# A fixed number of filler steps per attention slot, a moved fetch, and a new order of weight tiles ahead of the merge

## The chip, the core and the metric

The kernel runs on one core of a Trainium2 chip. Five engines with queues of their own work on it: TensorE (PE in the rows; its weight loads have rows of their own, PEld), VectorE (DVE), ScalarE (ACT), GpSimd (POOL) and SyncE (SP), which here mostly issues DMAs. The metric is the device time of one execution in microseconds, the median of several runs. Times in a profile are counted from the start of the span of one profiled execution.

## The reference, cut to what matters

One block of a conformer-like network, batch 1, 1024 tokens, width 1024, all in float32.

```
h = rms_norm(x, norm1_g);  z = h @ w_in                  # 1024 x 7168
glu_in, q, k, v, gate_logits = split(z)
a = a_val * sigmoid(a_gate)                              # from glu_in
a = silu(rms_norm(causal_depthwise_conv(a, 31 taps)))
y_a = a @ w_conv_out
q, k = rms_norm per head;  q *= 64 ** -0.5               # 16 heads of 64
for window, dilation in ((128, 1), (512, 4), (2048, 16)):
    o_g, lse_g = dilated_window_attention(q, k, v, slopes, window, dilation)
o = sum over g of softmax(lse)_g * o_g
y_b = o @ w_attn_out
g_a, g_b = split(sigmoid(gate_logits + gate_b))
x = x + (g_a * y_a + g_b * y_b) @ w_out
h = rms_norm(x, norm2_g)
u = causal_depthwise_conv(h @ w_up, 3 taps)
return x + (silu(u_gate) * u_val) @ w_down
```

## The kernel before

**Numbers as pairs.** Each float32 operand of a product is split into a high part, rounded to the type float32r by ACT (L83), and a low part, the difference, by DVE (L84). A product is then three matmuls: high x high, high x low, low x high. Weights are loaded by SP into a ring of four buffers, tag `raw` in `stage` (L88), and split into rings of four, `whi` and `wlo`. The rings are shared by everything that stages a tile, so a load waits until an older tile has been split or added.

**Who sets the order.** Blocks under `tc.manual_schedule` keep the order in which the code issues its instructions on ACT, DVE and PE. Everything else, all of SP's DMAs among it, is put in order by a planner when the program is built: an instruction goes out when the planner's own model of the run has its inputs and its buffer ready, earlier code first among those that are ready. On the chip each engine then works through its list strictly in that order. SP has eight DMAs in flight at most; the next one waits for the one eight places before.

**Stages.** First norm and gated convolution input; q, k and v (L132 to L134), spilled to DRAM; the convolution on DVE; then the gates of five pairs of channels by a Strassen-like scheme (`PAIRS`, the loop at L799 and on, products at L139 to L141), with copies out of PSUM into `quarter` buffers (five places in turn) that are written to `dgate` in DRAM; then the attention; then the merge with `w_attn_out`, the output product, and the feed-forward part from about 1100 us on.

**The attention loop.** A slot is one block of 128 queries of one head: 16 heads x 2 halves x 4 blocks, 128 slots, and six more behind. In each slot PE computes the scores (`score`, L887 and L888), issues filler steps, transposes the probabilities of a block five slots older (`flip`, L907, `BACK`), weighs the values with the transposes of the slot before (`weigh`, L921 and L922), and issues more filler steps. DVE adds the mask and finds the row extreme (L892), ACT takes the exponent (L897, in `powers`), and one slot later DVE and POOL divide by the sum (`share`, L900 and L901). ACT and DVE split each transpose into `ph` and `pl` (L83, L84). At the end of a half, `result` copies the output (L930) and writes it to `do_` in DRAM (L932). Later slots of a half have more keys: a score has 128 to 1024 columns.

**Filler steps.** `side_steps` (L195 and on) is a generator over work that does not depend on the attention: four late gate channels (`LATE`) and the eight output channels of `y_a`, in two halves each. One step is three matmuls of 512 columns (`gemm_half`, L115 to L117), eight steps make one half of a channel: (4 + 8) x 2 x 8 = 192 steps. `fill` advances the generator. Its weights are asked for two or three uses ahead, and their splits go through a queue of pieces, one or two a slot. What is left of the generator when the slots are done is issued in one go, the drain:

```
            for _ in gates:
                piece_low()
                piece_high()
```

**The merge.** `load_heads(half)` reads the attention's output back, two arrays per pair of chunks, adds them on DVE (L1008) and splits the sum into `oT`, whose memory lies where the attention's tiles were. `merge(c, w, half)` multiplies it with the tile `ao{c}` of `w_attn_out` and with the gates: channels 0 to 3 for half 0, then the same for half 1, then channels 4 to 7.

Of the kernel before, what the change touches and what calls it, by code (L numbers as in the profile page):

```python
# [32 lines left out]

LAG = 2
WARM = 7
FILL = (0.8, 2.2, 0.6, 0.6, 0.4, 1.7, 0.8, 0.9)
FIRST = 1.0
BACK = 5
SHARE = 0.6
PLAIN = (10, 11)  # L40
LATE = (12, 13, 14, 15)
PAIRS = ((0, 1), (2, 3), (4, 5), (6, 7), (8, 9))
# [15 lines left out]
def block_kernel(ctx: ExitStack, tc: tile.TileContext, x, xT, x0, g2, pack, mask,  # L58
# [27 lines left out]
    def stage(src, name):  # L86
        raw = wp.tile([P, 1024], F32, tag="raw", bufs=4, name=f"raw_{name}")
        sp.dma_start(raw.rearrange("p (a b) -> p a b", a=src.shape[1]) if len(src.shape) == 3 else raw, src)  # L88
        return raw
# [7 lines left out]
    def wpiece(src, name, raw=None):  # L97
        raw = stage(src, name) if raw is None else raw
        hi, lo = wsplit(raw, name)
        if len(src.shape) == 3:  # L100
            hi = hi.rearrange("p (a b) -> p a b", a=src.shape[1])
            lo = lo.rearrange("p (a b) -> p a b", a=src.shape[1])
        return hi, lo
# [45 lines left out]
    def fetch(dst, src):  # L149
        sp.dma_start(dst.bitcast(F32), src.bitcast(F32))  # L150
# [150 lines left out]
    if True:  # L301
# [431 lines left out]
        def head(h):  # L733
            hp, r, g8 = h // 2, (h % 2) * DH, h // 8
            q = p2.tile([P, T], F32R, tag="q", bufs=2, name=f"q_{h}")
            kh = p2.tile([P, T], F32R, tag="kh", bufs=2, name=f"kh_{h}")
            kl = p2.tile([P, T], F32R, tag="kl", bufs=2, name=f"kl_{h}")
            m = p2.tile([P, T], F32, tag="m", bufs=2, name=f"m_{h}")
            for s in range(2):
                fetch(q[s * DH : (s + 1) * DH, :], dq[g8][s][r : r + DH, hp % 4, :])  # L740
                fetch(kh[s * DH : (s + 1) * DH, :], dk[g8][0][r : r + DH, hp % 4, :])
                fetch(kl[s * DH : (s + 1) * DH, :], dk[g8][1][r : r + DH, hp % 4, :])
            sp.dma_start(m, mask[h])
            return q, kh, kl, m
# [6 lines left out]
        tiles = {}  # L751
        tt_ = lambda o, a, b, op: dve.tensor_tensor(out=o, in0=a, in1=b, op=op)

        def load(n, which):
            raws[n][which] = stage(w_ch[16 + PAIRS[n][which]], f"g{which}_{n}")
# [9 lines left out]
        def parts(n, which, name):  # L765
            src = raws[n][which] if which != "s4" else raws[n][0][:, 512:]
            pw[n][name] = [four(t) for t in wsplit(src, f"{name}_{n}")]
# [26 lines left out]
        with tc.manual_schedule(engines=hand):  # L794
            for n in range(2):
                xz[n] = gate_first(n, firsts[n])
                begun(n)
            load(1, 0)
            for n, (a, b) in enumerate(PAIRS):  # L799
                X = xz[n][:, 0:512]  # L800
                Y = bank_ps(f"gy_{n}")
                (sh, sl), (gh, gl) = pw[n]["s12"], pw[n]["s3"]
                inner = 0 < n < N - 1
                if n + 2 < N:
                    load(n + 2, 0)
                if n == 3:
                    p1_cm.__exit__(None, None, None)
                    p2_cm = tc.tile_pool(name="ph2", bufs=1, reuse_waits="tile")
                    p2 = p2_cm.__enter__()
                    pool2.append(p2)  # L810
                    tiles[0] = head(0)
                if n + 1 < N:
                    load(n + 1, 1)
                parts(n, "s4", "s4")
                if inner:
                    parts(n + 1, 0, "v")
                product(X, sh[:, 4:8], sl[:, 4:8], *form["t2"], False)
                c12 = quarter(f"c12_{n}")
                act.activation(c12, X, AF.Copy)
                product(Y, sh[:, 0:4], sl[:, 0:4], *form["t1"], True)  # L820
                p5 = quarter(f"p5_{n}")
                act.activation(p5, Y, AF.Copy)
                if n == 0:
                    rs8 = conv_factors()
                if n == 1:
                    conv_spread(rs8)
                if 0 < n < 3:
                    for c in range(4 * n - 4, 4 * n):
                        conv_result(c)
                product(X, gh[:, 0:4], gl[:, 0:4], *b12, False)  # L830
                c22 = quarter(f"c22_{n}")
                tt_(c22, X, p5, add)
                sp.dma_start(dgate[b][:, 512:1024], c22)
                if n + 1 < N:
                    sums(n + 1)
                if inner:
                    xz[n + 1] = big_ps(f"gx_{n + 1}")
                    for i in range(2):
                        product(xz[n + 1][:, i * 512 : i * 512 + 512], *(t[:, 4 * i : 4 * i + 4] for t in pw[n + 1]["v"]),
                                *left[i], True)  # L840
                    parts(n + 1, 2, "s12")
                    begun(n + 1)
                else:
                    product(Y, *pw[n]["s4"], *b22, False)
                    tt_(c12, Y, c12, add)
                    if n + 1 < N:
                        parts(n + 1, 2, "s12")
                product(X, gh[:, 4:8], gl[:, 4:8], *form["t4"], False)
                c21 = quarter(f"c21_{n}")
                act.activation(c21, X, AF.Copy)  # L850
                sp.dma_start(dgate[b][:, 0:512], c21)
                if inner:
                    product(Y, *pw[n]["s4"], *b22, False)
                if n + 1 < N:
                    parts(n + 1, 1, "s3")
                if inner:
                    tt_(c12, Y, c12, add)
                sp.dma_start(dgate[a][:, 512:1024], c12)
# [7 lines left out]
    if True:  # L866
# [64 lines left out]
            for i in range(2):  # L931
                sp.dma_start(do_[i][r : r + DH, h // 2, cs], tmp[i * DH : (i + 1) * DH, :])  # L932

        credit = [0.0]

        def fill(n):
            credit[0] += n
            while credit[0] >= 1.0:
                credit[0] -= 1.0
                next(gates, None)  # L940

        slots = [(h, half, n) for h in range(H) for half in range(2) for n in range(4)]
        pts = {}
# [7 lines left out]
        with tc.manual_schedule(engines={ENG.Activation, ENG.DVE, ENG.PE}):  # L953
            pend = []
            for at in range(len(slots) + BACK + 1):
                count[2] += 1
                cur = slots[at] if at < len(slots) else None
                rate = FILL[at % 8] + FIRST * (at < 6) if cur else 4
                if cur is not None:
                    h, half, n = cur  # L960
                    if (half, n) == (0, 2) and h + 1 < H:
                        tiles[h + 1] = head(h + 1)
                    if (half, n) == (1, 2) and h + 1 < H:
                        values(h + 1)
                    new = score(h, tiles[h], half * 4 + n)
                    pts[h, half, n] = new[0]
                if late is not None:
                    share(*late)
                if len(pieces) > 2:
                    piece_high(2)  # L970
                fill(rate * SHARE)
                flips = []
                if BACK <= at < len(slots) + BACK:
                    h, half, n = slots[at - BACK]
                    nkt = half * 4 + 4
                    row4 = [pts[h, half, i] for i in range(4)]
                    for kt in range(n * nkt // 4, (n + 1) * nkt // 4):
                        flips.append((h, half, vals[h], *flip(h, half, row4, kt)))
                for w in pend:
                    done = weigh(*w) or done  # L980
                pend = flips
                late = None
                if done is not None:
                    result(*done)
                    done = None
                if cur is not None:
                    powers(*new)
                    late = new
                piece_low()
                fill(rate * (1 - SHARE))  # L990
                piece_high(2)
            for _ in gates:
                piece_low()
                piece_high()
# [7 lines left out]
    if True:  # L1002
# [6 lines left out]
                split(oT[0][half][:, k : k + 2, :], oT[1][half][:, k : k + 2, :], raw.rearrange("p (a b) -> p a b", a=2))  # L1009

        load_heads(0)
        ao_raw = [stage(w_ao[c], f"ao{c}") for c in range(2)]
        load_heads(1)
        mT = hb_tiles(hb1, "mT")
        gb2 = p3.tile([P, D], F32, name="gb2")
# [36 lines left out]

        wo_first = []
        for c0 in (0, 4):
            ws = [wpiece(w_ao[c], f"ao{c}", ao_raw.pop(0) if ao_raw else None) for c in range(c0, c0 + 4)]
            for half in range(2):
                for c in range(c0, c0 + 4):
                    if c < 6 or not half:
                        merge(c, ws[c - c0], half)
# [553 lines left out]
```

## Time and profile before

| | |
|---|---|
| median of three runs | 1748.92 us (1747.99 to 1751.1) |
| the profiled execution | 1752.18 us, its span 1750.1 us |
| PE busy | 1733.1 us, 99% of the span |
| DVE, ACT, POOL busy | 1333.5, 812.6, 174.6 us |
| mean granted clock of PE | 0.998 of full speed |
| DMA over the span | 171 GB/s |

A row of the timeline gives start, duration, engine, line, operation, what is written and read, the shapes, and in brackets the idle time before it with what ended it. SPq and ACTq are DMA issues. Because matmuls are pipelined, a matmul's duration is longer than its distance to the next, and a busy PE can still be waiting for a fraction of a microsecond. Tile names leave their numbers out, so `p<-gy` of L822 is the copy `p5`. `gx` and `gy` are the gate pairs' PSUM tiles, `gate` and `ya` those of filler steps, `yb` that of the merge.

### The profile page before, as it was taken

To read this page: it belongs to the slowest core of one execution; us is meant where nothing else is said; L and a number is where in the kernel's file an instruction comes from. 1 tells how busy PE (TensorE), PEld (TensorE's weight loads), DVE (VectorE), ACT (ScalarE), POOL (GpSimd) and SP (SyncE) were. 2 spreads that over 40 slices of the span, in tenths; PEclk is the share of its full clock that TensorE was granted. 3 is DMA by queue.
4 is the path that set the end of the run, shared out by engine and by line. 5 is a ranking of instruction groups with operands and counts; after the bars stand their busy time and mean duration, and the time that the engine had idled before them with its cause. 6 is when DMAs were issued, how large, how long until landed. Compare 5 with 4: busy or idle time off the path is not lost.

```text
span 1750.1 us, 22916 instructions
## 1 busy us (share of the span) xinstructions
PE 1733.1 (99%) x8147; PEld 1440.5 (82%) x8147; DVE 1333.5 (76%) x2032; ACT 812.6 (46%) x1284; POOL 174.6 (10%) x188
## 2 busy tenths in 40 slices
PE   9999999999999899999999999999999999999999
PEld 7888888888878788888888888888888888888887
DVE  5999999999875467776755564787776777789863
ACT  5421233323444477877755442555544544544431
POOL 0000231131000133333310000000000000000000
PEclk9999999999999999999999999999999999999999
DMA  9311145345547768876749577632222222399851
GB/s 376 134 57 51 50 133 169 113 140 168 175 165 231 254 181 218 233 230 187 194 127 323 174 258 259 214 117 85 85 84 85 79 91 84 125 339 329 294 175 49
DMA packets 159842, 299.02 MB, mean 171 GB/s; under 512 B 13296, under 2 KB 63088, under 8 KB 159216
## 3 DMA queue, kind: packets, MB, share of 16 engines
q1 hardware_dynamic: 157280, 291.14, 51.2%
q10 hardware_dynamic: 2448, 6.42, 0.9%
q8 instruction: 64, 1.05, 0.2%
q14 instruction: 50, 0.41, 0.1%
HBM read 213.62 MB, written 83.89 MB: 170 GB/s over the span
## 4 chain that ended last, share of the span: by engine, by line
PE 93%; DMA 3%; DVE 2%; issue 1%; ACT 0%; SPq 0%; POOL 0%; ACTq 0%; DVEq 0%
PE dx L1425 7%; PE xz L139 6%; PE xz L141 6%; PE xz L140 6%; PE dy L1425 5%; PE qkv L134 5%; PE qkv L132 5%; PE qkv L133 5%; PE pp L907 4%; PE y L141 2%; PE y L139 2%; PE y L140 2%; PE o L922 2%; PE s L888 2%; PE s L887 2%; PE o L921 2%
## 5 line engine op out<-in xcount | busy, mean ns | idle before, releaser
L132 PE MATMUL qkv<-hi_qkv,hT 128*128 128x512 f32 x384 | 151.2, 395 | 0.0
L134 PE MATMUL qkv<-hi_qkv,hT 128*128 128x512 f32 x384 | 149.8, 391 | 0.0
L133 PE MATMUL qkv<-lo_qkv,hT 128*128 128x512 f32 x384 | 149.8, 391 | 0.0
L84 DVE TENSOR_TENSOR pl<-pp,ph 128x512 fp32r<-128x512 f32 (+2 forms) x191 | 99.5, 549 | 46.5 <-ACT ph L83 46.5
L1328 DVE SCALAR_TENSOR_TENSOR u<-u,pk 128x1023 f32<-128x1023 f32 x88 | 112.3, 1278 | 1.2 <-ACT u L1326 0.9
L901 POOL TENSOR_SCALAR p<-p,st 128x128 f32<-128x128 f32 (+3 forms) x120 | 89.3, 747 | 196.4 <-DVE st L900 137.2
L892 DVE CUSTOM_DVE_ANT_0 p<-s,m 128x128 f32<-128x128 f32 (+3 forms) x120 | 90.3, 753 | 24.1 <-PE pp L907 20.4
L83 ACT ACTIVATE ph<-pp 128x512 fp32r<-128x512 f32 (+2 forms) x191 | 86.3, 487 | 47.0 <-PE pp L907 43.4
L897 ACT ACTIVATE p<-p,st 128x128 f32<-128x128 f32 (+3 forms) x120 | 93.3, 778 | 20.1 <-DVE st L892 18.1
L108 POOL TENSOR_TENSOR rs<-ss,mhalf 128x8 f32<-128x8 f32 x32 | 66.9, 2092 | 294.2 <-DVE ss L107 294.2
L581 DVE SCALAR_TENSOR_TENSOR cacc<-csum,both,cacc 128x512 f32<-128x512 f32 x120 | 89.9, 749 | 0.3
L581 DVE SCALAR_TENSOR_TENSOR cacc<-apad,pk,cacc 128x512 f32<-128x512 f32 x120 | 88.8, 749 | 0.0
L84 DVE TENSOR_TENSOR lo_uv<-raw_uv,hi_uv 128x1024 fp32r<-128x1024 f32 x20 | 24.5, 1226 | 79.8 <-ACT hi_uv L83 79.8
L581 DVE SCALAR_TENSOR_TENSOR codd<-apad,pk,codd 128x513 f32<-128x513 f32 x112 | 84.2, 752 | 0.7 <-ACT codd L574 0.7
L134 PEld LDWEIGHTS qkv<-hi_qkv,hT 128*128 128x128 f32 x384 | 72.1, 188 | 15.0
L133 PEld LDWEIGHTS qkv<-lo_qkv,hT 128*128 128x128 f32 x384 | 72.2, 188 | 14.2
L132 PEld LDWEIGHTS qkv<-hi_qkv,hT 128*128 128x128 f32 x384 | 72.1, 188 | 14.2
L907 PE MATMUL pp<-ident,p 128*128 128x128 f32 x540 | 82.3, 275 | 1.4 <-POOL p L901 1.2
L907 PEld LDWEIGHTS pp<-ident,p 128*128 128x128 f32 x540 | 63.9, 140 | 15.4 <-POOL p L901 4.7
L921 PE MATMUL o<-ph,v 128*128 128x512 f32 (+2 forms) x191 | 74.1, 392 | 0.0
L922 PE MATMUL o<-pl,v 128*128 128x512 f32 (+2 forms) x191 | 66.0, 354 | 3.7 <-DVE pl L84 2.1
L139 PE MATMUL xz<-blk_t,hi_s3g 128*128 128x512 f32 x176 | 68.7, 390 | 0.0
(428 smaller groups left out, 4970.8 us busy)
## 6 DMA issues: line engine op xcount, KB each, us to landing
wr<-w_down SPq DMA_DIRECT2D x45, 512.0 KB, 5.7
gr<-dff SPq DMA_DIRECT2D x62, 256.0 KB, 5.2
raw_qkv<-w_qkv SPq DMA_DIRECT2D x24, 512.0 KB, 4.0
dff<-u SPq DMA_DIRECT2D x22, 512.0 KB, 2.6
raw_uv<-w_up SPq DMA_DIRECT2D x21, 512.0 KB, 3.2
raw_ug<-w_up SPq DMA_DIRECT2D x20, 512.0 KB, 3.2
raw_g<-w_ch SPq DMA_DIRECT2D x16, 512.0 KB, 4.1
dv<-v SPq DMA_DIRECT2D x16, 512.0 KB, 3.3
```

The source lines that it names most:

```text
L84: dve.tensor_tensor(out=lo, in0=src, in1=hi.bitcast(F32), op=ALU.subtract)
L132: pe.matmul(ps, ah, hi[:, k % 2, :], start=(k == 0), stop=False)
L133: pe.matmul(ps, ah, lo[:, k % 2, :], start=False, stop=False)
L134: pe.matmul(ps, al, hi[:, k % 2, :], start=False, stop=(k == KT - 1))
L139: pe.matmul(o, wh[:, k, :], bh[:, k, :], start=(start and k == 0), stop=False, skip_group_check=not start)
L140: pe.matmul(o, wh[:, k, :], bl[:, k, :], start=False, stop=False, skip_group_check=not start)
L141: end = pe.matmul(o, wl[:, k, :], bh[:, k, :], start=False, stop=(k == 3), skip_group_check=not start)
L581: dve.scalar_tensor_tensor(out=out_, in0=src[:, i : i + size], scalar=w(i), in1=out_, op0=ALU.mult, op1=ALU.add)
L907: pe.transpose(pp[:, qb * P : (qb + 1) * P], pts[qb][:, kt * P : (kt + 1) * P], ident)
L921: pe.matmul(o[:, c], v[:, kt, :], ph[:, c], start=(kt == 0), stop=False)
L1328: dve.scalar_tensor_tensor(out=acc[:, d:], in0=src[:, : T - d], scalar=w(2 - d), in1=acc[:, d:], op0=ALU.mult, op1=ALU.add)
L1425: pe.matmul(banks[n][:, cols], a[:, c], b[:, d], start=(start and i == 0 and m == 0), stop=(stop and i == nf - 1 and m == 2), skip_group_c ...
```

## The change

Three edits.

1. The fractional rates `FILL`, `FIRST` and `SHARE`, which were added up as credit, are replaced by two tuples of whole numbers, `FRONT` and `BEHIND`: steps ahead of the transposes and behind the weighing in each of the eight slots of a head, ten a head. In the six slots behind the last score both are 2, where a rate of 4 was shared 0.6 to 0.4.
2. In the gate pairs' loop the first head's fetches, `head(0)`, are issued behind `load(n + 1, 1)` of the same pass (n = 3) instead of ahead of it.
3. Ahead of `load_heads(1)`, four tiles of `w_attn_out` are now loaded and split (`wpiece`), where two were only loaded (`stage`) and split later.

```
-FILL = (0.8, 2.2, 0.6, 0.6, 0.4, 1.7, 0.8, 0.9)
-FIRST = 1.0
+FRONT = (1, 1, 0, 0, 0, 1, 0, 1)
+BEHIND = (1, 1, 1, 1, 0, 1, 1, 0)
 BACK = 5
-SHARE = 0.6
...
-                    tiles[0] = head(0)
                 if n + 1 < N:
                     load(n + 1, 1)
+                if n == 3:
+                    tiles[0] = head(0)
...
-        credit = [0.0]
-
         def fill(n):
-            credit[0] += n
-            while credit[0] >= 1.0:
-                credit[0] -= 1.0
+            for _ in range(n):
                 next(gates, None)
...
-                rate = FILL[at % 8] + FIRST * (at < 6) if cur else 4
+                front, behind = (FRONT[at % 8], BEHIND[at % 8] ) if cur else (2, 2)
...
-                fill(rate * SHARE)
+                fill(front)
...
-                fill(rate * (1 - SHARE))
+                fill(behind)
...
         load_heads(0)
-        ao_raw = [stage(w_ao[c], f"ao{c}") for c in range(2)]
+        ao_first = [wpiece(w_ao[c], f"ao{c}") for c in range(4)]
         load_heads(1)
...
-            ws = [wpiece(w_ao[c], f"ao{c}", ao_raw.pop(0) if ao_raw else None) for c in range(c0, c0 + 4)]
+            ws = [wpiece(w_ao[c], f"ao{c}") for c in range(c0, c0 + 4)] if c0 else ao_first
```

## The prediction

> **What bounds the kernel now.** I read the page first, for the engine that has no room.
>
> ```profile
> span 1750.1 us, 22916 instructions
> ...
> PE 1733.1 (99%) x8147; PEld 1440.5 (82%) x8147; DVE 1333.5 (76%) x2032; ACT 812.6 (46%) x1284; POOL 174.6 (10%) x188
> ```
>
> TensorE (PE) is busy 99% of the span, so work moved about on PE is worth nothing in itself; only PE's waits can be won or lost. Next I read the waits of PE alone (total, number, longest), and the busy time by stage (busy of each engine, granted clock).
>
> ```profile
> PE gy L139 <- ACT p L822: 4.6, 1, 4.6
> PE o L922 <- DVE pl L84: 2.1, 5, 0.4
> PE pp L907 <- POOL p L901: 1.2, 1, 1.2
> ...
> PE yb L117 <- DVE lo_ao L84: 0.4, 1, 0.4
> ```
>
> ```profile
> 550.00:600.00 50.00, 45.37 (x196) 37.21 (x195) 17.07 (x36) 16.15 (x30) 4.12 (x5) 0.93 0.85 257
> 600.00:900.00 300.00, 294.71 (x1701) 250.70 (x1699) 221.29 (x589) 223.39 (x514) 92.34 (x123) 1.00 0.73 199
> ```
>
> There are three places: one hole of 4.6 us ahead of the attention (a clock of 0.93 beside it), 5.3 us of visible idle in 300 us of attention, and a little at the merge. A matmul's row (0.39 us for 512 columns below) runs past the start of the next, 0.23 later, so short waits hide in "busy"; I found them as start-to-start distances in the timeline.
>
> The hole, in the chain that ended last (start, us, what):
>
> ```profile
> 559.98 12.22 DMA q<-dq
> 572.27 7.85 DMA dgate<-c
> 580.22 0.60 ACT p L822
> 580.87 0.80 PE gy L139
> 581.66 0.43 PE gy L140
> ...
> 588.89 0.23 PE gx L140
> ```
>
> The last pair's copy at L822 needs a quarter buffer, which is free when the previous pair's dgate write lands; that write was issued only at 572.27, behind head fetches. PE idles 4.63 us, then its twelve matmuls start 0.43 apart, not 0.23: 580.87 to 586.2 where 2.7 would do, 2.6 us more. The hole costs 7.2 us here.
>
> **Part 1, the fillers.** There are 192 steps (4 gate channels and 8 output channels, 2 halves, 8 steps each). The credits (rates that sum to 8.0 a head, 1.0 more in each of the first six slots, 4 in each of six slots behind the last score) give 14 in head 0, 8 in each later head, 24 behind, and leave 34 for the drain. The fixed tuples give 10 in every head, the same 24, and leave 8. So 26 steps of 0.7 us (first distance below) leave the drain for the slots: 18 us of PE on both sides, sum 0. What counts is where a step stands. As (front, behind), a steady head before is 00 21 00 01 00 11 01 01; after it is 11 11 01 01 00 11 01 10. Slot 0 gains one of each, slot 2 one behind, slot 1 loses a front one, slot 7's goes from behind to front. One head (slot 7, 0, 1), then a later slot 0:
>
> ```profile
> 641.10 1.22 DVE L892 CUSTOM_DVE_ANT_0 p<-s,m 128x1024 f32<-128x1024 f32 x1 [0.77 <-PE pp L907]
> ...
> 642.27 0.37 PE L921 MATMUL o<-ph,v 128*128 128x256 f32 x1
> ...
> 642.32 0.40 DVE L84 TENSOR_TENSOR pl<-pp,ph 128x256 fp32r<-128x256 f32 x1
> ...
> 642.78 0.39 PE L922 MATMUL o<-pl,v 128*128 128x256 f32 x1
> ...
> 643.97 1.47 POOL L901 TENSOR_SCALAR p<-p,st 128x1024 f32<-128x1024 f32 x2 [0.38 <-DVE st L900]
> ```
>
> ```profile
> 644.64 0.83 PE L907 MATMUL pp<-ident,p 128*128 128x128 f32 x4
> ```
>
> ```profile
> 645.15 0.76 PE pp L907 x5
> ```
>
> ```profile
> 737.01 0.37 PE L921 MATMUL o<-ph,v 128*128 128x256 f32 x1
> 737.82 0.39 PE L922 MATMUL o<-pl,v 128*128 128x256 f32 x1 [0.44 <-DVE pl L84]
> ```
>
> Slot 0: L922 starts 0.51 us after L921, where 256 columns take 0.12 (half of 0.23); 0.39 is a wait for pl. DVE computes pl behind the 1.22 us score reduction of slot 7, and that follows slot 7's score, not its transposes. So putting slot 7's step in front does not delay pl, while slot 0's front step holds the matmul back by 0.7: the wait goes. In four of the 15 heads (the second pair of rows) it is 0.69, about 0.67 of which is covered. 11 x 0.39 + 4 x 0.67 = **-7.0**.
>
> Slot 1 (the last two fences are the timeline and the chain): three transposes of 0.11 from 644.64 end at 644.97, the fourth starts at 645.15, when POOL has shared out the slot-7 score; 0.18 lost. Between that score and these transposes stand 3 steps before and 4 after, less the 0.39 just removed: 0.3 us more room. 15 x 0.16 = **-2.4** (bounds 0 and -2.7). No other distance in a steady head gets shorter.
>
> Head 0 loses four steps of cover. Its first transposes need the fourth score's share:
>
> ```profile
> 594.99 0.33 PE L887 MATMUL s<-kh,q 128*128 128x384 f32 x1
> ...
> 595.57 0.40 PE L115 MATMUL gate<-hT,hi_gt 128*128 128x512 f32 x1
> ...
> 596.27 0.39 PE L887 MATMUL s<-kh,q 128*128 128x512 f32 x1
> ...
> 596.97 0.40 PE L115 MATMUL gate<-hT,hi_gt 128*128 128x512 f32 x1
> ```
>
> ```profile
> 596.88 1.05 POOL L901 TENSOR_SCALAR p_first<-p_first,st 128x512 f32<-128x512 f32 x1 [1.13 <-DVE st L900]
> ```
>
> The share ends 2.94 after slot 4's score begins. PE then has after the change 0.58 (score) + 0.70 (score) + 0.70 (one step) + 0.33 (three transposes) = 2.31: **+0.6** (0 to 1.7).
>
> Weights: each is still asked two uses (16 steps, 1.6 heads) ahead, and the slots between hide its load and split: nothing. Without them a tile shows whole, 7.4 us by the merge's first (914.54 to 921.96 below). But the last conv weights are asked at step 136, now in head 13 and no longer at the end, so their raw buffers come free two heads sooner, and more of the late heads' adds (1.23 us of DVE) fall inside the loop. One such add stood ahead of the 1.2 us POOL wait listed above. Between -1.2 and +2.4, **0**.
>
> **Part 2, head(0).** It swaps program order of seven fetches and one weight load on SP, an engine that the planner orders by readiness.
>
> ```profile
> 542.95 1.23 DVE L84 TENSOR_TENSOR lo_s<-gs,hi_s 128x1024 fp32r<-128x1024 f32 x1 [2.16 <-ACT hi_s L83]
> ```
>
> ```profile
> 544.20 0.33 SPq L88 DMA_DIRECT2D raw_g<-w_ch  x1
> ...
> 549.53 0.51 SPq L150 DMA_DIRECT2D q<-dq  x1
> ```
>
> The load already goes out first, the moment DVE frees its buffer (544.18), 5.3 us ahead of the first fetch. I expect the same order and the same hole: **0**. If the write's path were cleared, -7.2; a loss could be the one issue (0.33, above) by which the fetches move back.
>
> **Part 3 and the lost cover.** At the end, with F = 906.73, the end of the last transposes:
>
> ```profile
> 906.49 0.49 PE L907 MATMUL pp<-ident,p 128*128 128x128 f32 x3
> ```
>
> ```profile
> 935.98 0.39 PE L115 MATMUL yb<-oT,hi_ao 128*128 128x512 f32 x1
> ```
>
> ```profile
> 908.26 2.36 DVE L84 TENSOR_TENSOR oT<-raw_o,oT 128x1024 fp32r<-128x1024 f32 x2 [3.20 <-ACT oT L83]
> ...
> 920.73 1.23 DVE L84 TENSOR_TENSOR lo_ao<-raw_ao,hi_ao 128x1024 fp32r<-128x1024 f32 x1
> ```
>
> ```profile
> 914.54 0.35 SPq L88 DMA_DIRECT2D raw_ao<-w_ao  x1
> ...
> 918.38 0.38 SPq L88 DMA_DIRECT2D raw_o<-do  x1
> ```
>
> ```profile
> 928.74 1.23 DVE L84 TENSOR_TENSOR lo_ao<-raw_ao,hi_ao 128x1024 fp32r<-128x1024 f32 x1 [0.87 <-ACT hi_ao L83]
> ...
> 948.28 1.22 DVE L84 TENSOR_TENSOR oT<-raw_o,oT 128x1024 fp32r<-128x1024 f32 x1
> ```
>
> The merge began at F+29.3; without 26 steps of 0.68 it can begin at F+11.5. Its first weights were split at F+15.2 (920.73+1.23). That load was issued at F+7.8, because half 0's late chunks waited for raw buffers; with those chunks mostly loaded before F, it goes out when the second chunk's split ends, F+3.9, and is split by F+11.3 to 12.2: **+0.5**. (If not moved: 3.8 us.) A third oT split can stand ahead of the last pl on DVE: half of its 1.2 us, **+0.5**. Weights two and three ahead of the merge remove the 0.4 us yb wait: **-0.35**. Half 1 of oT was ready at F+42.8 (948.28+1.22); it is wanted from F+33.3, its last chunk six steps later, F+37.4. Its first load now waits for ao0's buffer, F+12.3 and not F+11.7. But its fourth waited until F+23.2 for ao1's split, which stood behind the drain (928.74+1.23); now it follows ao3's (load behind the last half-0 split, F+11, and 7.4 us for the tile), near F+19, and the rest comes forward with it by 4: ready near F+38.5, **+1.0** (0 to 8.7). The new order adds a wait on ACT: the splits of ao2 and ao3 need high-weight buffers that the last two filler channels hold until eight steps and no step ahead of the merge, F+6 and F+11.5. Behind them on ACT stand half 1's splits, whose data land from F+17 on: nothing; PE waits for neither before its third channel, 11 us later.
>
> **The sum.** -7.0 - 2.4 + 0.6 + 0 + 0 + 0.5 - 0.35 + 0.5 + 1.0 = -7.15. The profiled execution took 1752.18 us (span and 2.1 around it), 3.3 above the median of the runs, 1748.92: it would give 1745.0, and the median **1741.8**.
>
> [...]
>
> **The rivals.**
> - *The cover was needed* (slower). One mechanism: half 1's loads behind four weight tiles. Two more tiles hold raw buffers for 7.4 us each, two of them at a time: 7.4 on F+42.8, F+50.2 against F+37.4, 12.8 us of waiting in place of my 1.0: 1753.6. Spread over all four buffers it would be half, 1749.9; from F+49 on the change is slower. For it: the loads of half 1 took 31 us, and 26 are left. Against: the wait for ao1's split that goes.
> - *The last-pair hole goes too.* A wait of 4.6 less in the median: 1737.2; 1734.6 with the clock. For it: the chain names head fetches. Against: the order on SP shown above.
> - *The slots keep their waits* (the change does not do this). If pl and the shares move along with the steps, terms one and two are 0: 1751.2. Against: pl follows the score reduction.
>
> **How the numbers follow.** Forecast 0.54 (1738 to 1746), hole gone 0.14, cover needed 0.20, slots unchanged 0.12. A difference of 0.2%, 3.5 us, is about what a measurement of this kernel can tell from none (its three runs span 3.1): faster is below 1745.4, slower above 1752.4. Faster: 0.14 and 0.51 of the forecast, 0.65; same: the unchanged slots, the forecast's upper edge 0.03 and 0.03 of the cover case, 0.18; slower: the rest of that, 0.17. The range reaches into the neighbours on both sides, to 1734 and 1752.5, and leaves out the worse part of the cover case.
>
> **What would show it.** Right: in slot 0 L921 and L922 0.12 apart with a step between score and transpose; heads 19.6 us apart (before, 642.27 to 737.01 is five heads, 18.9 each; + 1.4 - 0.65); the hole at L822 as before; eight ya steps, then yb within 1 us. Wrong: a gap ahead of the first yb or of yb's second half, above all one over 3 us with a half clock behind it; new POOL or DVE waits in the loop; another SP order near 549.

## The result, and the profile after

| | before | after |
|---|---|---|
| median, first set of runs | 1748.10 us (12 runs, 1745.95 to 1751.12) | 1747.79 us (12 runs, 1740.99 to 1751.32) |
| ratio, first set | | 0.9997, interval 0.9984 to 1.0010 |
| the profiled execution | 1752.18 us, span 1750.1 | 1749.37 us, span 1747.6 |
| median, three later sets | 1750.18 (29 runs), and 1750.25 (23 runs) for the last two | 1744.29, 1746.30, 1745.76 |
| ratio of three later sets | | 0.9966 (0.9954 to 0.9978), 0.9981 (0.9971 to 0.9992), 0.9979 (0.9968 to 0.9989) |

The first set shows no difference. The three later sets, run beside the experiments, show the changed kernel 0.2 to 0.3% faster. The four ratios have a mean of 0.998, some 3.4 us. The forecast was 7.15 us. Where did the other half go? (The kernel before moved as well: 1748.10 in the first set, 1750.2 to 1750.5 in all later ones. About half of the step from the first ratio to the later ones is that first set of before.)

The page after, and the waits of PE (total, number, longest). The edits move the line numbers: after the change ACT's split is L82, DVE's L83, a step L114 to L116 and the add of the late heads L1002; the variants below shift them again by a few lines.

```profile
span 1747.6 us, 22903 instructions
PE 1727.9 (99%) x8147; PEld 1440.1 (82%) x8147; DVE 1332.8 (76%) x2032; ACT 811.4 (46%) x1284; POOL 175.8 (10%) x188
```

```profile
PE pp L907 <- DVE pl L83: 5.4, 2, 3.3
PE gy L138 <- ACT p L822: 3.4, 1, 3.4
PE yb L114 <- ACT hi_ao L82: 1.7, 1, 1.7
...
PE pp L907 <- POOL p L901: 0.8, 1, 0.8
```

The hole at L822 is still there. Two waits are new: 5.4 us for `pl` in the attention, and 1.7 us ahead of the merge. By stretches (columns as in the prediction), first the steady part of the attention, before and after, then two heads near its end, before and after:

```profile
590.00:840.00 250.00, 246.19 (x1418) 209.26 (x1417) 185.11 (x500) 187.61 (x432) 79.06 (x105) 1.00 0.77 209
```

```profile
590.00:840.00 250.00, 248.51 (x1437) 214.17 (x1436) 184.51 (x493) 185.30 (x429) 79.18 (x103) 1.00 0.75 208
```

```profile
840.00:890.00 50.00, 48.53 (x279) 41.41 (x278) 37.91 (x98) 36.85 (x85) 15.16 (x21) 1.00 0.55 157
```

```profile
840.00:890.00 50.00, 44.59 (x254) 37.89 (x252) 32.22 (x84) 31.16 (x73) 13.01 (x18) 0.97 0.61 175
```

In the steady part 2.3 us more of PE's work fit into the same 250 us, on top of the short waits hidden inside "busy"; by the length of its heads it got what was forecast, as the section on why the prediction was right or wrong shows. In the two heads from 840 us on PE lost 3.9 us of busy time against before, and its clock fell to 0.97. DVE shows why (timeline of DVE after), and the chain that ended last passes through the same place (start, us, what):

```profile
868.58 0.69 DVE L83 TENSOR_TENSOR pl<-pp,ph 128x512 fp32r<-128x512 f32 x1
872.40 1.23 DVE L1002 TENSOR_TENSOR raw_o<-raw_o,raw_o 128x1024 f32<-128x1024 f32 x1 [3.12 <-DMA raw_o<-do]
873.54 0.55 DVE L83 TENSOR_TENSOR pl<-pp,ph 128x384 fp32r<-128x384 f32 x1
```

```profile
866.02 6.36 DMA raw_o<-do
872.87 0.67 issue
873.54 0.56 DVE pl L83
877.66 0.85 PE pp L907 x4
```

The add of the late heads' chunk 4 (L1002; chunks come in pairs, 0, 2, 4 and 6) stands on DVE between two splits of transposes. Its second load was issued at 866.02 and landed 6.36 us later. DVE came to the add 3.12 us before that and stood still, the next `pl` behind it, and PE's transposes behind that `pl`. Chunk 2's add, at 851.54, waited 1.84 us in the same way. Three adds stand in the loop after the change; the first, at 835.00, waited for nothing. Before, two stood in it, and the longer of their waits was 0.62 us:

```profile
870.54 1.31 DVE L1008 TENSOR_TENSOR raw_o<-raw_o,raw_o 128x1024 f32<-128x1024 f32 x1 [0.62 <-DMA raw_o<-do]
```

The three DVE rows show DVE keeping its order here: it is idle for 3.12 us at the add, with a split behind it whose high part ACT had finished by 868.93.

The second new wait, in PE's timeline:

```profile
932.27 0.39 PE L114 MATMUL yb<-oT,hi_ao 128*128 128x512 f32 x1
932.50 0.39 PE L115 MATMUL yb<-oT,hi_ao 128*128 128x512 f32 x1
934.57 0.50 PE L114 MATMUL yb<-oT,hi_ao 128*128 128x512 f32 x1 [1.69 <-ACT hi_ao L82]
934.91 0.40 PE L115 MATMUL yb<-oT,hi_ao 128*128 128x512 f32 x1
935.15 0.39 PE L116 MATMUL yb<-oT,lo_ao 128*128 128x512 f32 x1
```

A step is L114, L115, L116. Here the order is 114, 115, 114, 115, 116: in the built program the planner, which orders PE in the merge, has put two matmuls of the *second* output channel ahead of the first channel's third. This foreign pair waits for the second tile's high part:

```profile
931.78 1.23 DVE L83 TENSOR_TENSOR lo_ao<-raw_ao,hi_ao 128x1024 fp32r<-128x1024 f32 x1 [0.37 <-ACT hi_ao L82]
...
933.46 1.06 ACT L82 ACTIVATE hi_ao<-raw_ao 128x1024 fp32r<-128x1024 f32 x1 [1.72 <-DMA raw_ao<-w_ao]
```

The first tile's low part was ready at 933.00, the second tile's high part at 934.52.

To see which stage each kernel wins or loses in, I cut the span at three rows of PE's timeline: the first transpose, the first product of the merge (`yb`) and the first output product (`wo`). The missing edges of before, and those of after (its `yb` edge is above):

```profile
598.36 0.27 PE L907 MATMUL pp<-ident,p_first 128*128 128x128 f32 x1
...
1023.68 0.39 PE L132 MATMUL wo<-hi_wo,mT 128*128 128x512 f32 x1
```

```profile
594.27 0.27 PE L907 MATMUL pp<-ident,p_first 128*128 128x128 f32 x1
...
1021.29 0.39 PE L131 MATMUL wo<-hi_wo,mT 128*128 128x512 f32 x1
```

In this table the attention stage runs from the first transpose to the first `yb`, the merge stage from there to the first `wo`. All times are in us, of one profiled execution each. What follows the first `wo` takes 726.2 to 726.5 in all but tiles_only. "Windows" counts stretches of 3.41 us at half clock (a granted clock of 0.50) inside the attention stage.

| kernel | to first transpose | attention | windows | merge |
|---|---|---|---|---|
| before | 598.36 | 337.62 | 0 | 87.70 |
| after | 594.27 | 338.00 | 1 | 89.02 |
| again, again2, again3 (the same kernel) | 590.42, 590.04, 595.18 | 336.64, 339.44, 335.30 | 1, 2, 0 | 88.73, 88.33, 88.81 |
| hold, hold2 | 594.12, 594.76 | 331.08, 331.52 | 0, 0 | 88.56, 88.64 |
| slot0 | 593.34 | 341.57 | 0 | 89.04 |
| pe | 594.76 | 340.46 | 2 | 87.51 |
| place | 587.29 | 337.15 | 0 | 88.60 |
| holdplace | 587.56 | 331.43 | 0 | 88.77 |
| all3 | 587.16 | 331.14 | 0 | 87.54 |
| no_tiles | 593.47 | 337.32 | 1 | 106.05 |
| tiles_only | 597.28 | 337.90 | 0 | 87.04 |

Four steps of the slots (11 before, 7 after, ahead of the first transpose) moved out of the first column into the second; at 0.69 us each that is 2.8. So the attention went from 337.6 + 2.8 = 340.4 to 338.0 in the profiled pair, 2.4 less, where the prediction's slots alone said 8.8 less.

### The profile page after: what moved, and what is told of

Read it like the earlier page. It is cut to its first block, busy times and chain, and to the rows that moved or that the text cites. A ratio compares the mean times of both kernels' runs of the same rounds, so it can differ in the third digit from the quotient of the medians.

```text
span 1747.6 us, 22903 instructions
## 1 busy us (share of the span) xinstructions
PE 1727.9 (99%) x8147; PEld 1440.1 (82%) x8147; DVE 1332.8 (76%) x2032; ACT 811.4 (46%) x1284; POOL 175.8 (10%) x188
## 4 chain that ended last, share of the span: by engine, by line
PE 92%; DMA 4%; DVE 2%; issue 1%; ACT 0%; SPq 0%; POOL 0%; DVEq 0%; ACTq 0%; POOLq 0%
PE dx L1419 7%; PE xz L139 6%; PE xz L138 6%; PE xz L140 6%; PE dy L1419 5%; PE qkv L131 5%; PE qkv L133 5%; PE qkv L132 5%; PE pp L907 3%; PE y L139 2%; PE y L140 2%; PE y L138 2%; PE o L922 2%; PE s L888 2%; PE o L921 2%; PE s L887 2%
## 5 line engine op out<-in xcount | busy, mean ns | idle before, releaser
L83 DVE TENSOR_TENSOR pl<-pp,ph 128x512 fp32r<-128x512 f32 (+2 forms) x191 | 99.9, 550 | 46.5 <-ACT ph L82 46.0
L82 ACT ACTIVATE ph<-pp 128x512 fp32r<-128x512 f32 (+2 forms) x191 | 86.8, 489 | 83.8 <-PE pp L907 82.4
L83 DVE TENSOR_TENSOR lo_uv<-raw_uv,hi_uv 128x1024 fp32r<-128x1024 f32 x20 | 24.5, 1226 | 79.8 <-ACT hi_uv L82 79.8
L138 PE MATMUL xz<-h2left,hi_uv 128*128 128x512 f32 x176 | 68.6, 390 | 0.0
```

What stands on the lines that cost most here:

```text
L83: dve.tensor_tensor(out=lo, in0=src, in1=hi.bitcast(F32), op=ALU.subtract)
L138: pe.matmul(o, wh[:, k, :], bh[:, k, :], start=(start and k == 0), stop=False, skip_group_check=not start)
```

## The experiments

Each ratio is against the kernel before, run beside it. "The four sets" are the changed kernel's own, 1744.29 to 1747.79 us.

**hold: the late heads' adds come later on DVE.** Chunk 2's add is put behind the score reduction of slot 110, chunk 4's behind that of slot 118, two and three slots later than the planner had them.

```
+HELD = {2: 110, 4: 118}
...
-            dve.tensor_tensor_reduce(out=pt, in0=s[:, :nk], ...
+            reds[h * 8 + i] = dve.tensor_tensor_reduce(out=pt, in0=s[:, :nk], ...
...
-                dve.tensor_tensor(out=raw, in0=raw, in1=low, op=ALU.add)
+                with ExitStack() as held:
+                    if not half and k in HELD:
+                        held.enter_context(tc.issue_after(reds[HELD[k]].ins))
+                    dve.tensor_tensor(out=raw, in0=raw, in1=low, op=ALU.add)
```

> The changed kernel, with the late heads' adds of chunks 2 and 4 held back on DVE by two and three slots, so that their second load has landed when DVE reaches them; nothing else is edited. Theory A (the missing gain went into DVE standing still ahead of these adds, with the transposes' splits queued behind): PE's two waits for pl, 5.4 us, go, and the half-clock window behind them, worth half of 3.4, goes too: about 7 us less than the changed kernel's 1747.8, so 1740.7 and a ratio of 0.996 to the kernel before; heads 13 and 14 then take 19.6 us like the others. Rival (it is the 1.23 us of each add that DVE has no room for, wherever it stands): the wait moves with the add, 1747.8 and 1.000.

Measured: 1741.81 us, ratio 0.9949 (0.9936 to 0.9963), 2.5 to 6.0 us below the four sets. Inside the loop the waits for `pl` and DVE's waits for `raw_o` are gone. The two heads' stretch, which had 44.59 us of PE's work and a clock of 0.97, is full:

```profile
840.00:890.00 50.00, 49.97 (x291) 42.73 (x290) 36.56 (x98) 35.22 (x84) 14.39 (x21) 1.00 0.61 178
```

Heads 13 and 14, from the first score of head 13 to that of head 15, take 46.95 us after the change and 39.92 here:

```profile
837.22 0.22 PE L887 MATMUL s<-kh,q 128*128 128x128 f32 x1
...
884.17 0.23 PE L887 MATMUL s<-kh,q 128*128 128x128 f32 x1
```

```profile
837.00 0.22 PE L890 MATMUL s<-kh,q 128*128 128x128 f32 x1
...
876.92 0.22 PE L890 MATMUL s<-kh,q 128*128 128x128 f32 x1
```

Theory A holds, and the rival falls: the adds take the same 1.22 us of DVE and cost little where their data has landed. Not quite nothing: two undisturbed heads take 39.1, so each of these is still 0.4 longer, where the expectation had them like the others. What takes the 0.4 is open.

**pe: the merge in channel order.** Within half 0, each channel's products are placed behind the last product of the channel before, on PE.

```
-            pe.matmul(o, lo[:, k, :], ah[:, k, :], start=False, stop=(k == KT - 1))
+            ends[:] = [pe.matmul(o, lo[:, k, :], ah[:, k, :], start=False, stop=(k == KT - 1))]
...
+            with ExitStack() as turn:
+                if last_mm and not half:
+                    turn.enter_context(tc.issue_after(last_mm[-1].ins))
-            for _ in gemm_half(yp, w, oT, half):
-                pass
+                for _ in gemm_half(yp, w, oT, half):
+                    pass
+            last_mm.append(ends[-1])
```

> The changed kernel, with the merge's products of half 0 held to channel order on PE, so that two matmuls of the second channel no longer stand ahead of the first channel's third. Theory: the 1.7 us wait in the first channel was for the second channel's high weights (ready 934.52), not for its own low weights (ready 933.00); in channel order 0.3 us of wait is left: 1.4 us less, 1746.4, ratio 0.999. Rival: the first channel's third matmul is late by itself, and the wait stays at 1.7: 1747.8, 1.000. By time alone the two are hardly told apart; the wait in the trace tells them.

Measured: 1746.83 us, 0.9982 (0.9971 to 0.9993), inside the spread of the changed kernel's own sets. In the trace the wait is 0.2 us, for `lo_ao`, and the merge stage 87.51 against 88.3 to 89.0. So the wait was the foreign pair's; by time alone this run does not show it, as expected.

**no_tiles: without the third part.**

```
-        ao_first = [wpiece(w_ao[c], f"ao{c}") for c in range(4)]
+        ao_raw = [stage(w_ao[c], f"ao{c}") for c in range(2)]
...
-            ws = [wpiece(w_ao[c], f"ao{c}") for c in range(c0, c0 + 4)] if c0 else ao_first
+            ws = [wpiece(w_ao[c], f"ao{c}", ao_raw.pop(0) if ao_raw else None) for c in range(c0, c0 + 4)]
```

> The changed kernel without its third part: two tiles of w_attn_out loaded ahead of half 1's loads and the other two behind them, as before. Theory (with the fixed fillers the third part is needed, since the drain of 34 steps that hid the late tiles is gone): the third channel's tile is issued only behind half 1's last load, near 952, and split near 960, while PE wants it near 943 and has 4 us of half 1 to do first: some 10 us of waiting, 1757, ratio 1.005. Rival 1 (the third part changes nothing but the order of loads): 1747.8, 1.000. Rival 2, from the prediction's cover case (its two more tiles delay half 1): faster than the changed kernel, by up to 8.7 us.

Measured: 1764.50 us, 1.0081 (1.0065 to 1.0096). PE waits for the third and fourth tile, whose loads go out at 951.03 behind half 1's last; half of the clock goes with it (PE's waits, SP's timeline, and a stretch of the wait):

```profile
PE yb L114 <- ACT hi_ao L82: 16.4, 2, 14.7
```

```profile
949.89 0.37 SPq L87 DMA_DIRECT2D raw_o<-do  x1
951.03 2.68 SPq L87 DMA_DIRECT2D raw_ao<-w_ao  x2
```

```profile
949.10:962.50 13.40, 3.89 (x9) 2.87 (x10) 9.14 (x9) 6.72 (x8) 0.00 (x0) 0.50 0.88 312
```

The loss was 17 to 20 us against the four sets, more than the 10 expected: the longer wait alone is 14.7, PE did none of the 4 us of half 1 that were expected ahead of it, and the first products behind it ran at half clock (0.50 up to 962.5). With the drain gone the third part is needed; the two rivals fall.

**place: the last pair's copy goes to a place that is free.** `quarter` has five places in turn. For the last pair, p5 takes the fifth place, and the later copies take the places that p5 and its neighbours leave.

```
-        def quarter(name):
+        def quarter(name, place=None):
             i = turn[0] = (turn[0] + 1) % 5
+            i = i if place is None else place
...
-                p5 = quarter(f"p5_{n}")
+                p5 = quarter(f"p5_{n}", 4 if n == N - 1 else None)
...
-                c22 = quarter(f"c22_{n}")
+                c22 = quarter(f"c22_{n}", 0 if n == N - 1 else None)
...
-                c21 = quarter(f"c21_{n}")
+                c21 = quarter(f"c21_{n}", 3 if n == N - 1 else None)
```

> The changed kernel, with the last pair's p5 copied to the place whose write landed at 569.5 and not to the one whose write lands at 579.7 (the third and the fifth copy of this pair take the places of writes landed by 577.3 and 579.7 in return). Theory (the hole is the wait for that one write): PE's 3.4 us wait at L822 goes and with it the half-clock window of 3.4 us behind it, worth 1.7: 5.1 us less, 1742.7, ratio 0.997. Rival (the transfers there are saturated and the next wait ends as late): the wait turns up at the third copy or at the gates' weights, and no more than 2 us are won: 1746, 0.999.

Measured: 1742.07 us, 0.9952 (0.9937 to 0.9968), 2.2 to 5.7 us below the four sets. No wait for L822 is left and none takes its place; the first transposes start at 587.29, 2.8 to 7.9 us earlier than in the four profiles of the changed kernel. DMA is as busy there as it was (a share of 1.00 from 550 to 590 us, 0.96 before this edit), so here it was one write that set the limit and not the sum of the transfers.

**again: the changed kernel beside the others.**

> The changed kernel itself, once more, beside the others: 0.9997 as before, within the interval 0.998 to 1.001. If it comes out at 0.998, the single runs' gains beyond the waits that they took away (8.4 against 7.1 us, 7.9 against 5.1, 2.6 against 1.4) are the baseline's and not the edits'.

Measured: 1744.29 us, 0.9966 (0.9954 to 0.9978). This is neither the 0.9997 of the first set nor the 0.998 that would have explained the surplus: the intervals of two sets of one kernel do not meet.

**slot0: slot 0's front step moved behind.**

```
-FRONT = (1, 1, 0, 0, 0, 1, 0, 1)
-BEHIND = (1, 1, 1, 1, 0, 1, 1, 0)
+FRONT = (0, 1, 0, 0, 0, 1, 0, 1)
+BEHIND = (2, 1, 1, 1, 0, 1, 1, 0)
```

> The changed kernel with slot 0's front step moved behind the weighing (FRONT 0, BEHIND 2 in slot 0; still ten steps a head). Theory (the prediction's first term: this step alone covers the wait for pl): the wait comes back, 11 x 0.39 + 4 x 0.67 = 7.0 us more, 1754.8, ratio 1.004; L921 and L922 of slot 0 stand 0.51 apart again. Rival (pl is early now, since slot 7's step stands ahead of the transposes): no difference, 1747.8 and 1.000.

Measured: 1752.41 us, 1.0019 (1.0010 to 1.0028), 8.1 above the changed kernel run beside it and 4.6 above the slowest of the four sets. Slot 0's pair in a steady head, after and in slot0:

```profile
640.74 0.36 PE L921 MATMUL o<-ph,v 128*128 128x256 f32 x1
640.95 0.28 PE L922 MATMUL o<-pl,v 128*128 128x256 f32 x1
```

```profile
640.01 0.39 PE L921 MATMUL o<-ph,v 128*128 128x256 f32 x1
640.47 0.38 PE L922 MATMUL o<-pl,v 128*128 128x256 f32 x1
```

The distance goes from 0.21 to 0.46, not quite the 0.51 of before, and the attention stage grows by 6 us once the half-clock windows (1.7 each, an estimate, half of 3.41) are taken out of the others, by 6.7 once the late heads' waits for `pl` (3.9 here) are taken out of all; 7.0 was expected. The rival falls.

**all3: adds held, place and channel order together.** The three edits above.

> The changed kernel with three edits together: the late heads' adds held back by two and three slots, the last pair's p5 in an earlier place, and half 0 of the merge in channel order on PE. Theory (three separate waits, each ended by another transfer): the effects add up. By the waits of the changed kernel 7.1, 5.1 and 1.4 us, 13.6 less than 1747.8: 1734.2, ratio 0.992; by the three single runs' ratios against the changed kernel's 0.9997, 0.9949 x 0.9952 x 0.9982 / 0.9997 / 0.9997 = 0.989. PE shows no wait above 1 us. Rival (the waits share their cause, saturated transfers: with the hole gone all heads come 5 us earlier and the adds' second loads don't): part of a wait comes back, ratio 0.995, with PE waiting for pl again in heads 13 and 14.

Measured: 1735.37 us, 0.9921 (0.9907 to 0.9934). That is near the 1734.2 that the waits gave, and not the 0.989 of the single ratios. Against the changed kernel it is 12.4 us less than the first set, from which the 1734.2 was reckoned, but 8.9 less than the set run beside it. The share of the span, and the longest of PE's waits that are left:

```profile
PE 1724.6 (100%) x8147; PEld 1437.6 (83%) x8147; DVE 1332.8 (77%) x2032; ACT 810.9 (47%) x1284; POOL 175.3 (10%) x188
```

```profile
PE early L464 <- POOL ones L343: 1.0, 1, 1.0
PE pp L913 <- POOL p L907: 1.0, 2, 0.8
```

The first stands outside the attention and the merge. No wait for `pl` came back, so the rival falls, and this version is faster than both kernels.

**tiles_only: the third part alone, on the kernel before.**

```
-        ao_raw = [stage(w_ao[c], f"ao{c}") for c in range(2)]
+        ao_first = [wpiece(w_ao[c], f"ao{c}") for c in range(4)]
...
-            ws = [wpiece(w_ao[c], f"ao{c}", ao_raw.pop(0) if ao_raw else None) for c in range(c0, c0 + 4)]
+            ws = [wpiece(w_ao[c], f"ao{c}") for c in range(c0, c0 + 4)] if c0 else ao_first
```

> The kernel before with the third part alone (four tiles of w_attn_out ahead of half 1's loads). Theory (the old drain of 34 steps hides the tiles in either order): the 0.4 us wait at yb goes and nothing comes, 1747.7, ratio 0.9998. Rival (the prediction's cover case, two more tiles delay half 1's loads by 7.4 us): PE waits in half 1 of the merge, 3 to 7 us, ratio 1.002 to 1.004.

Measured: 1748.43 us, 0.9993 (0.9983 to 1.0003): nothing, as the theory said. The merge stage is 0.7 us shorter, and a 1.2 us wait for the first `wo` weights stands behind it, outside the stages that the change touches:

```profile
PE wo L133 <- DVE lo_wo L1047: 1.2, 1, 1.2
```

**again2, again3: the changed kernel twice more, side by side.**

> The changed kernel once more: two sets of runs gave 0.9997 and 0.9966, whose intervals do not meet. View A (the time of this kernel differs from one loading to the next by more than the interval of one set, by the size of the hole at L822, which was 1.5 to 4.6 us in eight profiles of the same instructions): a third and a fourth set lie between or beside the two, 0.9966 to 0.9997, and differ from each other. View B (the first set was the odd one): both at 0.9966 within 0.001.

> The same kernel as the run before it, loaded once more, on the same chip: view A expects another value between 0.9966 and 0.9997, view B 0.9966.

Measured: 1746.30 us, 0.9981 (0.9971 to 0.9992), and 1745.76 us, 0.9979 (0.9968 to 0.9989). Both lie between the first two sets, as view A said, and agree with each other, which it had not said. View B falls, by little: they lie 0.0013 and 0.0015 from its 0.9966, where it allowed 0.001. What made the first two sets differ is not settled. Of the some 5.5 us between them, 3.5 is the changed kernel's and 2.1 the kernel before's, which was at 1748.10 beside the first set and at 1750.18 beside the second. A part of the 3.5 is under the last heading.

**hold2: the held adds once more, beside them.**

> The kernel with the late heads' adds held back, once more. Theory A: by the stage from the first to the last transpose it saves 5.6 to 6.9 us against the changed kernel (319.9 against 325.4 and 326.8), so it should lie that far below the mean of the changed kernel's sets of this call, ratio 0.994 to 0.995, and its stage at 319.9 again. Rival (the 2.5 us by which it lay below one set is all that it is worth): 2 to 3 us below the sets of this call.

Measured: 1741.43 us, 0.9949 (0.9933 to 0.9966), 4.3 to 4.9 below the two sets run beside it, with the attention at 331.52. That lies between the rival's 2 to 3 and the theory's 5.6 to 6.9, nearer to the theory's. Its profile held the longest hole at L822 of all the changed kernel's relatives, 4.3 us.

**holdplace: all3 without the channel order.**

> The kernel with three edits without the merge's channel order: adds held back and p5 in an earlier place. Theory: the foreign pair's wait of 1.2 to 1.7 us is back and nothing else, 1736.5, ratio 0.993 against 0.992 with all three; the stage from the first product of the merge to the first output product is 88.6 and not 87.5 us. Rival (channel order costs elsewhere what it saves, since the kernel with it alone was not faster than the changed kernel): 0.992 or below.

Measured: 1736.10 us, 0.9924 (0.9910 to 0.9938). The wait of 1.4 us for `hi_ao` is back and the merge stage 88.77, against 87.54 in all3. The two times, 0.7 apart, cannot be told apart; the trace says that the order saves 1.2.

## Why the prediction was right or wrong

The range (1734 to 1752.5) held the time, but it is 18.5 us wide and holds no change at all as well. The central value, 1741.8, was 6 us too low by the first set and 2.5 to 4.5 by the later ones. The first set shows no difference, to which the prediction gave 0.18; it gave 0.65 to a faster kernel, which the later sets show, by less than forecast.

- **Slots 0 and 1, and head 0 (-7.0, -2.4, +0.6): right.** Where the adds do not disturb it, the attention stage takes 331.1 to 331.5 us against 340.4, about 9.1 less, where these terms say 8.8. A steady head takes 19.56 us, forecast 19.6:

```profile
641.75 0.28 PE L887 MATMUL s<-kh,q 128*128 128x256 f32 x1
...
661.31 0.28 PE L887 MATMUL s<-kh,q 128*128 128x256 f32 x1
```

  Over heads 1 to 12 the mean is 19.71 after and 18.97 before, with two steps (1.38) more: 0.64 won a head, 0.63 forecast. It is not the same in all of them. Heads 6 to 8 take 20.8, 19.9 and 19.8, the first with a wait of 0.82 for POOL's `p`, one of the prediction's signs of being wrong. The split between the two terms is not the forecast's either. Slot 0's pair stands 0.21 apart, not 0.12: pairs of this shape are 0.20 apart, before and after, where the profile shows no wait, so the wait to be won was about 0.3 and not 0.39. That the front step covers it, slot0 shows. Head 0's fourth transpose starts 1.03 behind the first, where three take 0.33, so its wait is 0.7, forecast 0.6:

```profile
594.27 0.49 PE L907 MATMUL pp<-ident,p_first 128*128 128x128 f32 x3
595.30 0.33 PE L907 MATMUL pp<-ident,p_first 128*128 128x128 f32 x1 [0.54 <-POOL p_first L901]
```

- **The late heads' adds ("Between -1.2 and +2.4, 0"): wrong, and this is where the gain went.** That the adds would come earlier was seen; they were priced as DVE work, 1.23 us each. What they cost is DVE's standing still for a transfer. In four profiles of the changed kernel the attention took 335.3 to 339.4 us, with the adds held 331.1 and 331.5: 4 to 8 us, of which 4.1 to 5.4 is waiting for `pl` and 1.7 (an estimate, half of 3.41) each half-clock window. With both taken out the four lie at 330.8 to 331.2, so nothing is left over. The bound should have been a landing time, not a busy time: the load on the chain took 6.36 us, and nothing but the planner's order keeps DVE from coming to the add first.
- **Part 2 (0): right.** SP issues the load and the first fetch in the same order as before, 5.0 us apart (5.3 before):

```profile
545.29 0.33 SPq L87 DMA_DIRECT2D raw_g<-w_ch  x1
...
550.30 0.51 SPq L149 DMA_DIRECT2D q<-dq  x1
```

  The hole stayed. Its length was called 4.6 us by one profile; in the eleven profiles in which p5's place was not changed it was 1.3 to 4.6, and behind it came no half-clock window, one, or two.
- **The merge's start (+0.5 and +0.5) and its later weights (-0.35): sizes off.** The first tile was split at 933.00, F + 11.7 (F, the last transposes' end, is 921.3), within the forecast's F + 11.3 to 12.2. But the forecast took the merge to run in channel order. The foreign pair made the wait 1.7, and the merge stage 1.3 longer than before. The other +0.5, a third `oT` split ahead of the last `pl`, did not come: the last `pl` starts at 921.90, the three `oT` splits at 923.01, behind it.
- **Half 1 (+1.0): right in time by luck.** Its last split ended at F + 44.7 and not F + 38.5, near the bad end of the bound, and yet PE never waited: the same free order on PE took the early chunks of all four channels first. DVE reads half 0's last product at 956.21 and half 1's first only 17 us later, and then two more within 4.2 us:

```profile
973.44 0.69 DVE L1029 TENSOR_TENSOR gg<-yb,gg 128x512 f32<-128x512 f32 x1 [6.84 <-PE yb L116]
975.91 0.68 DVE L1029 TENSOR_TENSOR gg<-yb,gg 128x512 f32<-128x512 f32 x1
977.64 0.68 DVE L1029 TENSOR_TENSOR gg<-yb,gg 128x512 f32<-128x512 f32 x1
```

  The prediction's working, in channel order, would have made that a loss of some 7 us (F + 37.4 against F + 44.7).
- **The rivals.** "The cover was needed" had the sign of part 3 wrong: its mechanism, half 1's loads behind four tiles, leaves PE no wait, and without the four tiles the kernel loses 17 to 20 us. The prediction credited the third part with 0.35 us, since it never asked what the shorter drain would do to the old order of tiles. "The last-pair hole goes too" did not happen, but place shows that it can be had. "The slots keep their waits" is shown false by slot0.
- **Luck.** The adds took 4 to 8 us out of the gain, and yet the later sets miss the forecast's 7.15 by only 1 to 3. In the profiles part of the loss is made up ahead of the attention: with the four moved steps counted, the changed kernel reaches its first transpose 0.4 to 5.5 us earlier than the kernel before, where the prediction had 0. The kernel before with part 3 alone (tiles_only) reaches it 1.1 earlier too, so how much of this is the change's stays open.

## What to carry to other kernels

Here an add of 1.23 us on DVE also cost the 3.12 us until its load had landed, and the splits queued behind it waited with it. So when an edit lets a load's consumer move forward into a tight loop, bound it by the load's issue-to-landing time (6.36 us here), and not by the consumer's busy time. Place such a consumer by hand some slots after its load; there it cost 0.4 us a head here, not 2.5 and 5.3. And look in the timeline for instructions of another tile between the steps of one accumulation: here PE's wait of 1.69 us at the merge was for such a pair, which could have come later.

## What the runs showed of the hardware

**Half clock behind waits shorter than the stretch.** The half-clock stretches were 3.41 us long, or 6.83 (at the 4.63 us hole of the kernel before) and 13.65 (at the 14.7 us wait of no_tiles). A wait of 2.75 us (again2) was followed by one, and a wait of 3.53 us (place) by none; for each, PE's row that ends the wait, and the stretch behind it (the clock is the third number from the end):

```profile
871.54 0.47 PE L907 MATMUL pp<-ident,p 128*128 128x128 f32 x1 [2.75 <-DVE pl L83]
```

```profile
871.30:874.60 3.30, 3.06 (x10) 2.68 (x11) 1.51 (x6) 1.08 (x3) 0.70 (x1) 0.50 0.00 0
```

```profile
867.91 0.33 PE L908 MATMUL pp<-ident,p 128*128 128x128 f32 x1 [3.53 <-DVE pl L83]
```

```profile
868.00:872.00 4.00, 4.00 (x24) 3.52 (x25) 2.62 (x9) 2.22 (x6) 1.50 (x2) 1.00 0.02 4
```

Of PE's waits for `p` at L822 and for `pl` or POOL's `p` in the attention, in all profiles here, none up to 2.1 us was followed by a stretch, 12 of the 15 from 2.4 to 3.7 us were, and all three from 4.2 to 4.6 us were, two of them by 6.83 us. So here the length of a wait on PE says only how likely a half-clock stretch is, and a wait need not be as long as the stretch: one of 3.41 us came behind 2.75. Each stretch of 3.41 us costs 1.7 us, an estimate from its clock of 0.50.

**The spread of the changed kernel's runs went with the clock.** In the changed kernel's first set the time went with the mean granted clock: 1740.99 us at a clock of 1.000, a mean of 1747.5 at 0.998, 1750.9 at 0.996. At 1.000 the second set had 1740.5. The first set had a mean clock of 0.9978 and the second 0.9987, a difference of about one stretch of 3.41 us at half clock (0.001 of the span), which is part of the 3.5 us between their medians, not all of it. The kernel holdplace, with two of the three waits removed, ran at 1.000 in all its five runs, within 2.2 us; all3, with all three removed, had two of its six runs at 0.999 and a spread of 3.2. The changed kernel's sets spread over 5.5 to 10.3 us, in 11 or 12 runs each. So a wait here cost more than it showed where a half-clock stretch followed, 1.7 us by the estimate above, and the kernel with the waits was harder to measure: one set's interval (0.9984 to 1.0010) was too narrow for another set of the same kernel (0.9966).
